# A gated delta rule loop: a second buffer for a unit's score blocks, longer delays in the rule that orders TensorE's work, keys queued ahead of values

## The chip, the cores and the metric

The kernel runs on one core of a Trainium2 chip. The metric is the device time of one execution in microseconds. The time before is the median of three runs.

## What is computed

A trunk of two layers over 1024 tokens of width 1024. Layer 0 mixes tokens with gated linear attention, layer 1 with a gated delta rule, and a dense SwiGLU network follows each. The change touches the mixer of layer 1 alone. Per chunk and head it computes this (cut from the reference):

```python
kb = kc * bc[..., None]
A = jnp.where(strict, jnp.einsum('bhid,bhjd->bhij', kb, kc) * decay, 0.0)
T = lax.linalg.triangular_solve(eye + A, eye, left_side=True, lower=True)
v_new = T @ (vc * bc[..., None]) - T @ (kb * jnp.exp(G)[..., None]) @ S
o = (qc * jnp.exp(G)[..., None]) @ S + (where(causal, qc @ kc.T * decay, 0)) @ v_new
S = jnp.exp(G_last) * S + k_dec.T @ v_new
```

There are 8 key heads, and two value heads for each. The inputs of the chunks come from projections with a short causal convolution, and the gated output goes through an output projection that is added to the residual.

## The kernel before

The mixer works in 16 **units**: a unit is one key head (its two value heads with it) over one half of the tokens, 512 of them in four chunks of 128. Units 0 to 7 are the first half, 8 to 15 the second. One unit goes through these steps, each a small generator in the code:

- `keys` and `values` project and convolve q, k and two blocks of v; `late` projects the gate z. A projection is 24 matmuls of 512 columns with split weights (`whi`, `wlo`; GpSimd makes `wlo` in L169).
- `prep` makes the decays and the score blocks `nt` (L834 to L843: four matmuls of k with itself, `pp<-k`, then eight VectorE operations), and the blocks `at` for the output.
- `solve` inverts the diagonal 32 by 32 blocks of `nt`. It sends them through DRAM (`d1`, L866) into the tile `nbx` (L868), lets VectorE do 31 steps of two operations (L883, L885), and sends the result through DRAM (`d2`, L893) into `xt` (L896). There is one `nbx` and one `xt`.
- `join` builds the whole inverse `tt` from the blocks: a transposition on VectorE (`xd`, L906), four groups of matmuls (`pq<-xd,nt` first, `pq<-ya,rr` last) with copies or additions between them, the last in L934. It reads `nt`, which until then cannot be overwritten.
- `seq` runs the four chunks in order through the state; `post` normalizes the output (L1035), transposes it (`pq<-cst,o`) and gates it; `out` projects it.

`prep` asks for the event `joined[n - 1]` before it makes `nt`, of which there is one buffer. So the score blocks of a unit are begun after the unit ahead has been joined.

What sets the order: TensorE's instructions stand in the order in which the class `Order` records them. It keeps a clock that each recorded matmul moves forward by a set amount. The strands `seq`, `post`, `join`, `prep`, `inputs` and `solve` are asked first, in this order; a strand that has yielded a number of microseconds or an event is skipped until the clock is there. When none can go on, the strand `dense` (the projections) gives one piece of three matmuls. So each `yield 1.5` says how long the rule supposes that the other engines take. The other engines and the DMA queue get their order from the framework's scheduler, which follows on from TensorE's. Every engine works through its own list in order.

Of the kernel before, what the change touches and what calls it, by code (L numbers as in the profile page):

```python
# [14 lines left out]
F32 = mybir.dt.float32  # L15
# [7 lines left out]
P = 128  # L23
# [72 lines left out]
class Trunk:  # L96
# [482 lines left out]
    def gdn(self):  # L579
# [5 lines left out]
        with ExitStack() as es:  # L585
# [75 lines left out]
            O = self.order  # L661
# [84 lines left out]
            def dense():  # L746
                yield from keys(0)
                yield from values(0)
                yield from late(0)
                yield from keys(1)  # L750
                yield from late(1)
                yield from keys(2)
                yield from values(1)
                for m in range(1, UN):
                    yield from values(m + 1)
                    if m + 2 in (NQ, UN):
                        yield from late(m + 1)
                        O.set(free[1 if m + 2 == NQ else 2])
                        yield from out(m - 1)
                        if m + 2 == NQ:  # L760
                            yield ready[1]
                            yield from keys(NQ)
                    else:
                        yield from keys(m + 2)
                        yield from out(m - 1)
                        yield from late(m + 1)
                yield ready[2]
                yield from self.headparts(1, mx, ("v", "v", "raw"))
                yield from out(UN - 1)
# [34 lines left out]
            def prep(n):  # L804
                half, hq = divmod(n, NQ)
                u = U[n]
                yield gated[half]
                gt = gts[half]
                yield keyed[n]
                yield from norms(n)  # L810
                yield 4.0
                q, k = u["q"], u["k"]

                dec = mx.tile([P, 2, C, P], F32, name="dec", tag="t1")
                up = self.upper.unsqueeze(1).to_broadcast([P, C, P])
                for h2 in range(2):
                    rhs = []
                    for nm in ("ghi", "glo"):
                        gs = gt[nm].bitcast(F32)[:, :, 2 * hq + h2:2 * hq + h2 + 1].to_broadcast([P, C, P])
                        rh = mx.tile([P, C, P], F32R, name="rh", tag="t2", bufs=2)  # L820
                        G.tensor_tensor(out=rh, in0=up, in1=gs, op=ALU.mult)
                        rhs.append(rh)
                    yield 3.0
                    ps = self.prepps()
                    psv = cview(ps)
                    self.mm(psv, self.cut, self.gt.unsqueeze(1).to_broadcast([P, C, P]), True, False)
                    self.mm(psv, self.gt, rhs[0], False, False)
                    self.mm(psv, self.gt, rhs[1], False, True)
                    S.activation(dec[:, h2].rearrange("p c i -> p (c i)"), ps, AF.Exp)
                yield 1.5  # L830
                if n:
                    yield joined[n - 1]

                nt = mx.tile([P, 8, P], F32, name="nt", tag="nt")  # L834
                pk = self.prepps()
                for c in range(C):
                    sl = slice(c * P, (c + 1) * P)
                    self.mm(pk[:, sl], k[:, sl], k[:, sl])
                for h2 in range(2):
                    for c in range(C):  # L840
                        V.scalar_tensor_tensor(out=nt[:, h2 * C + c, :], in0=pk[:, c * P:(c + 1) * P],
                                               scalar=u["nb2"][:, h2, c:c + 1], in1=dec[:, h2, c, :],
                                               op0=ALU.mult, op1=ALU.mult)  # L843
                O.set(scored[n], 4.0)
                u["nt"] = nt
                yield 2.0
                if n >= 2:
                    yield passed[n - 2]
                u["at"] = at = mx.tile([P, 8, P], F32, name="at", tag="at", bufs=2)
                ps = self.prepps()  # L850
                for c in range(C):
                    sl = slice(c * P, (c + 1) * P)
                    self.mm(ps[:, sl], k[:, sl], q[:, sl])
                for h2 in range(2):
                    V.tensor_tensor(out=at[:, h2 * C:(h2 + 1) * C, :], in0=cview(ps), in1=dec[:, h2], op=ALU.mult)

            def solve(n):
# [16 lines left out]
                G.memset(xi, 0.0)  # L874
                for b in range(4):
                    G.memset(xi[b * B:(b + 1) * B, b::B + 4], 1.0)
                yield 6.0
                start = O.clock + 0.75
                xv = xix[:, half].rearrange("p m i -> p i m")
                for s in range(B - 1):  # L880
                    m, w = B - 1 - s, s // 4 + 1
                    tv = tmpx[:, 0:m * w].rearrange("p (i m) -> p i m", m=w)
                    V.tensor_tensor(out=tv, in0=nbx[:, s, s + 1:].unsqueeze(2).to_broadcast([P, m, w]),  # L883
                                    in1=xv[:, s:s + 1, 0:w].to_broadcast([P, m, w]), op=ALU.mult)
                    V.tensor_tensor(out=xv[:, s + 1:, 0:w], in0=xv[:, s + 1:, 0:w], in1=tv, op=ALU.add)  # L885
                    yield O.until(start + 0.75 * s)

                if n:
                    yield joined[n - 1]
# [9 lines left out]
            def join(n):  # L899
# [5 lines left out]
                xd = mx.tile([P, 8, P], F32, name="xd", tag="t3")  # L905
                V.transpose(xd.rearrange("p a b -> p (a b)"), xt.rearrange("p a b -> p (a b)"))  # L906
                S.copy(tt, xt)
                yield 2.5

                rr = mx.tile([P, 8, P], F32, name="rr", tag="t4")  # L910

# [8 lines left out]
                for h2 in range(2):  # L920
                    S.copy(rr[:, hs[h2], :], quad(nt, xd, h2))
                    yield 0.5
                yield 1.5
                for h2 in range(2):
                    V.tensor_tensor(out=up(tt, h2, 96), in0=up(tt, h2, 96), in1=quad(rr, xt, h2, n=96), op=ALU.add)
                    yield 0.5
                yield 1.5
                ya = mx.tile([96, 8, P], F32, name="ya", tag="t3")
                for h2 in range(2):
                    S.copy(up(ya, h2, 96), quad(rr, tt, h2, n=96))  # L930
                    yield 0.5
                yield 1.2
                for h2 in range(2):
                    V.tensor_tensor(out=up(tt, h2, 64), in0=up(tt, h2, 64), in1=quad(rr, ya, h2, kn=96, n=64), op=ALU.add)  # L934
                U[n]["tt"] = tt
                O.set(joined[n], 1.5)

            def seq(n):
                half, hq = divmod(n, NQ)
# [89 lines left out]
            def post(n):  # L1029
                u = U[n]  # L1030
                yield passed[n]
                o, ss = u["o"]
                rs = self.rstd(ss.rearrange("p c h -> p (c h)"), 2 * C, P)
                for h2 in range(2):
                    V.tensor_tensor(out=o[:, :, h2, :], in0=o[:, :, h2, :], op=ALU.mult,  # L1035
                                    in1=rs[:, h2:2 * C:2].unsqueeze(2).to_broadcast([P, C, P]))
                yield 5.0
                yield gating[n]
                u["oT"] = []
                for h2 in range(2):  # L1040
                    ps = self.seqps()
                    self.turn(ps, lambda c: o[:, c, h2, :])
                    u["oT"].append(self.gateout(mx, h2, ps, self.gdnw, u["z"][:, h2, :]))
                O.set(posted[n], 4.0)
# [347 lines left out]
```

## Time and profile before

| | us |
|---|---|
| time, median of 3 runs (3480.7 to 3481.96) | 3481.23 |
| the profiled execution | 3478.09 |
| its span, first to last instruction | 3476.3 |
| the delta rule mixer, from the first score blocks to the last transposed output | 1347.6 to 2767.7 |
| one unit, from one join to the next, in the steady part | 85.2 to 89.2 |

The profiled execution is 1.8 us longer than its span and 3.1 us under the median. Times in the rows count from the start of the span. TensorE appears as PE (matmuls) and PEld (weight loads), VectorE as DVE, ScalarE as ACT, GpSimd as POOL, the DMA queue of SyncE as SP or SPq.

### The profile page before, as it was taken

Reading aid. Unit: us, or ns where it says so; the run is one execution under the profiler, and the core shown is the slowest. Engines: PE = TensorE matmul, PEld = TensorE weight load, DVE = VectorE, ACT = ScalarE, POOL = GpSimd, SP = SyncE. Lnnn points to the kernel's source line nnn. Section 1 sums busy time; section 2 is a strip of 40 time slices with the busy share of each in tenths; the row PEclk is TensorE's granted clock in tenths of the full one; section 3 lists DMA queues with packets and bytes.
Section 4 is the critical chain, followed back from the end, with each engine's and each line's share of the span. In section 5 each row is a group of like instructions: output and inputs, shape, how many; then the busy total and the mean of one; then the engine's idle time right before and its main releaser. Section 6 shows DMA issues by size and latency. Waiting matters only on the chain.

```text
span 3476.3 us, 40951 instructions
## 1 busy us (share of the span) xinstructions
PE 3016.6 (87%) x14547; PEld 2482.9 (71%) x14547; DVE 2065.9 (59%) x4212; ACT 1390.3 (40%) x2513; POOL 1522.6 (44%) x1037
## 2 busy tenths in 40 slices
PE   7988999799998988688888885888888879999898
PEld 5877877588876776566666674666667758888676
DVE  6465565623229866666666677666666463232888
ACT  4354444433433335343333453444443433433333
POOL 4344444455548744133223232333333345555875
PEclk9999999899999999799999998999999989999899
DMA  3221222322224202122222121222222232221431
GB/s 123 73 62 49 73 61 85 104 85 79 85 70 158 88 21 80 32 56 57 60 60 59 49 69 43 59 61 64 58 61 60 82 89 86 85 81 55 147 126 55
DMA packets 364923, 256.39 MB, mean 74 GB/s; under 512 B 67848, under 2 KB 309967, under 8 KB 364719
## 3 DMA queue, kind: packets, MB, share of 16 engines
q1 hardware_dynamic: 364654, 253.77, 24.4%
q8 instruction: 114, 1.87, 0.2%
q14 instruction: 91, 0.74, 0.1%
q0 software_dynamic: 64, 0.02, 0.0%
HBM read 219.12 MB, written 34.60 MB: 73 GB/s over the span
## 4 chain that ended last, share of the span: by engine, by line
PE 63%; DVE 26%; issue 4%; DMA 3%; ACT 2%; POOL 1%; SPq 1%; DVEq 0%; POOLq 0%; ACTq 0%
PE pd L201 36%; PE pq L201 14%; PE pp L201 8%; DVE tmpx L883 4%; DVE xix L885 3%; DVE alo L1274 2%; DVE h L1284 1%; DVE s L1268 1%; PE pp L207 1%; DVE v L692 1%; PE pp L484 1%; PE pq L207 1%; DVE k L692 1%; DMA ra<-act 1%; DVE q L692 1%
## 5 line engine op out<-in xcount | busy, mean ns | idle before, releaser
L169 POOL TENSOR_TENSOR wlo<-raw,whi 128x1024 fp32r<-128x1024 f32 x204 | 489.8, 2403 | 855.1 <-ACT whi L168 837.4
L201 PE MATMUL pd<-xhi,whi 128*128 128x512 f32 x1072 | 458.6, 428 | 1.2 <-ACT part L1082 0.9
L201 PE MATMUL pd<-xhi,wlo 128*128 128x512 f32 x1072 | 431.1, 402 | 1.9 <-POOL wlo L169 1.9
L201 PE MATMUL pd<-xlo,whi 128*128 128x512 f32 x1072 | 428.2, 399 | 0.0
L168 ACT CAST whi<-raw 128x1024 fp32r<-128x1024 f32 x204 | 213.1, 1045 | 229.7 <-PE pd L201 117.5
L1118 POOL TENSOR_TENSOR olo<-s,ohi 128x512 fp32r<-128x512 f32 x152 | 196.0, 1291 | 206.3 <-ACT ohi L1117 206.3
L1118 POOL TENSOR_TENSOR olo<-raw,ohi 128x512 fp32r<-128x512 f32 x138 | 190.7, 1384 | 201.4 <-ACT ohi L1117 177.3
L201 PEld LDWEIGHTS pd<-xhi,wlo 128*128 128x128 f32 x1072 | 206.8, 193 | 50.0 <-POOL wlo L169 2.8
L201 PEld LDWEIGHTS pd<-xhi,whi 128*128 128x128 f32 x1072 | 207.5, 194 | 36.9 <-ACT part L1082 2.0
L201 PEld LDWEIGHTS pd<-xlo,whi 128*128 128x128 f32 x1072 | 207.9, 194 | 35.6
L201 PE MATMUL pd<-whi,ohi 128*128 128x512 f32 x384 | 171.0, 446 | 43.5 <-DVE h L316 23.1
L1117 ACT CAST ohi<-s 128x512 fp32r<-128x512 f32 x152 | 94.3, 622 | 231.3 <-PE pd L201 174.7
L883 DVE TENSOR_TENSOR tmpx<-nbx,xix 128x60 f32<-128x60 f32 (+24 forms) x496 | 177.7, 358 | 8.5
L316 DVE TENSOR_TENSOR h<-h,pd 128x512 f32<-128x512 f32 x192 | 130.8, 683 | 62.9 <-PE pd L201 62.8
L1117 ACT CAST ohi<-raw 128x512 fp32r<-128x512 f32 x138 | 85.1, 621 | 197.6 <-POOL olo L1118 176.6
L201 PE MATMUL pd<-wlo,ohi 128*128 128x512 f32 x384 | 163.7, 426 | 0.0
L201 PE MATMUL pd<-whi,olo 128*128 128x512 f32 x384 | 161.8, 421 | 0.9 <-DVE olo L346 0.9
L885 DVE TENSOR_TENSOR xix<-xix,tmpx 128x60 f32<-128x60 f32 (+24 forms) x496 | 153.2, 309 | 8.7
L201 PE MATMUL pq<-xd,nt 128*128 128x128 f32 x256 | 57.3, 400 | 114.0 <-DVE xd L906 114.0
L1274 POOL TENSOR_TENSOR blo<-t,bhi 128x1536 fp32r<-128x1536 f32 (+1 forms) x32 | 124.7, 3896 | 57.4 <-ACT bhi L1273 53.0
L1226 DVE TENSOR_TENSOR p<-p,pp 128x512 f32<-128x512 f32 x38 | 26.1, 688 | 195.9 <-DMA raw<-in_ffn_w_gate_up_dram 148.3
L201 PE MATMUL pd<-bhi,ahi 128*128 128x512 f32 x264 | 108.3, 410 | 39.2 <-DVE h L1284 24.5
(393 smaller groups left out, 8261.2 us busy)
## 6 DMA issues: line engine op xcount, KB each, us to landing
raw<-in_gdn_w_in_dram SPq DMA_DIRECT2D x96, 512.0 KB, 4.0
raw<-in_ffn_w_gate_up_dram SPq DMA_DIRECT2D x176, 256.0 KB, 3.3
raw<-in_gla_w_in_dram SPq DMA_DIRECT2D x48, 512.0 KB, 3.8
ra<-act SPq DMA_DIRECT2D x88, 256.0 KB, 4.9
rb<-in_ffn_w_down_dram SPq DMA_DIRECT2D x24, 768.0 KB, 6.2
raw<-in_gdn_w_out_dram SPq DMA_DIRECT2D x32, 512.0 KB, 3.8
act<-p SPq DMA_DIRECT2D x44, 256.0 KB, 2.0
act<-u SPq DMA_DIRECT2D x38, 256.0 KB, 2.0
```

Source lines behind the costliest of these rows:

```text
L168: nc.scalar.copy(hi, raw)
L169: nc.gpsimd.tensor_tensor(out=lo, in0=raw, in1=hi.bitcast(F32), op=ALU.subtract)
L201: self.nc.tensor.matmul(out, lhsT, rhs, start=start, stop=stop, **kw)
L207: self.nc.tensor.transpose(ps[:, c * P:(c + 1) * P], src(c), self.ident)
L316: self.nc.vector.tensor_tensor(out=o, in0=o, in1=ps, op=ALU.add)
L484: TE.matmul(ps[:, sl], d[:, sl], d[:, sl], start=True, stop=True)
L692: V.scalar_tensor_tensor(out=out, in0=raw[:, s:s + HT], scalar=tap(s), in1=out, op0=ALU.mult, op1=ALU.add)
L883: V.tensor_tensor(out=tv, in0=nbx[:, s, s + 1:].unsqueeze(2).to_broadcast([P, m, w]), in1=xv[:, s:s + 1, 0:w].to_broadcast([P, m, w]), op= ...
L885: V.tensor_tensor(out=xv[:, s + 1:, 0:w], in0=xv[:, s + 1:, 0:w], in1=tv, op=ALU.add)
L1117: self.nc.scalar.copy(hi, src)
L1118: eng.tensor_tensor(out=lo, in0=src, in1=hi.bitcast(F32), op=ALU.subtract)
L1274: eng.tensor_tensor(out=lo, in0=src, in1=hi.bitcast(F32), op=ALU.subtract)
```

## The change

It does four things, all in the function of the delta rule mixer.

1. `nt` gets two buffers, and `prep` of unit n asks for `joined[n - 2]` where it asked for `joined[n - 1]`.
2. The numbers in `solve`, `join` and `post` grow: 6.0 to 9.0 before the steps, 0.75 to 1.1 for a step, 2.5 to 4.0 behind the transposition, 1.5 to 2.5 twice and 1.2 to 2.5 inside the join, 1.5 to 2.5 behind it, 5.0 to 8.0 ahead of the output's transpositions. This alters no instruction, only where TensorE's stand.
3. In the strand `dense`, `values(m + 1)` moves from the first to the third place of a round, behind the keys of unit m + 2 and the output projection of unit m - 1 (not in the last round of a half).
4. Nothing is added or removed: every engine does the same operations.

```diff
                 for m in range(1, UN):
-                    yield from values(m + 1)
                     if m + 2 in (NQ, UN):
+                        yield from values(m + 1)
                         yield from late(m + 1)
...
                         yield from keys(m + 2)
                         yield from out(m - 1)
+                        yield from values(m + 1)
                         yield from late(m + 1)
...
-                if n:
-                    yield joined[n - 1]
+                if n >= 2:
+                    yield joined[n - 2]
-                nt = mx.tile([P, 8, P], F32, name="nt", tag="nt")
+                nt = mx.tile([P, 8, P], F32, name="nt", tag="nt", bufs=2)
...
-                yield 6.0
-                start = O.clock + 0.75
+                yield 9.0
+                start = O.clock + 1.1
...
-                    yield O.until(start + 0.75 * s)
+                    yield O.until(start + 1.1 * s)
...
-                O.set(joined[n], 1.5)
+                O.set(joined[n], 2.5)
...
-                yield 5.0
+                yield 8.0
                 yield gating[n]
```

From line 763 on, the changed file's line numbers are higher by one.

TensorE's list before, at the end of the join of unit 4: the last group of the join, the transposed values and keys of that unit, and behind them the score matmuls `pp<-k` of unit 5.

```order
L201 MATMUL pq<-ya,rr 64x64 x8
L207 MATMUL pp<-cst,v_13533 128x128 x4
L207 MATMUL pp<-cst,v_13622 128x128 x4
L207 MATMUL pq<-cst,k 128x128 x4
L201 MATMUL pp<-k 128x128 x4
```

TensorE's list after: the score matmuls of unit 6 stand inside the first group of the join of unit 5, a whole join earlier, and the transposed outputs (`pq<-cst,o`) of unit 4 directly behind.

```order
L201 MATMUL pq<-xd,nt 128x128 x4
L201 MATMUL pp<-k 128x128 x4
L201 MATMUL pq<-xd,nt 128x128 x4
L207 MATMUL pq<-cst,o 128x128 x8
L201 MATMUL pd<-xhi,whi 128x512
```

The score matmuls have moved by one join; in the second half of the tokens they stand directly ahead of that first group in some units.

VectorE's list before, from the transposition of the solved blocks to the first step of the next solve:

```order
L906 STREAM_TRANSPOSE xd<-xt 128x1024
L925 TENSOR_TENSOR tt<-tt,pq 96x4x96 x2
L934 TENSOR_TENSOR tt<-tt,pq 64x4x64 x2
L961 TENSOR_TENSOR vt<-pp,sk 128x512 x2
L841 SCALAR_TENSOR_TENSOR nt<-pp,nb_13984,dec 128x128 x8
L855 TENSOR_TENSOR at<-pp,dec 128x512 x2
L999 COPY gstate_9876<-pq 128x256
...
L883 TENSOR_TENSOR tmpx<-nbx,xix 128x31
```

VectorE's list after, over the same stretch:

```order
L907 STREAM_TRANSPOSE xd<-xt 128x1024
...
L1036 TENSOR_TENSOR o<-o,rs_y 128x4x128 x2
L692 SCALAR_TENSOR_TENSOR v_14014<-raw,col_conv,v_14014 128x512
L842 SCALAR_TENSOR_TENSOR nt<-pp,nb_13797,dec 128x128 x8
L344 SCALAR_TENSOR_TENSOR sz<-pq,col_rest,sz 128x512 x2
...
L856 TENSOR_TENSOR at<-pp,dec 128x512 x2
L926 TENSOR_TENSOR tt<-tt,pq 96x4x96 x2
L935 TENSOR_TENSOR tt<-tt,pq 64x4x64
L884 TENSOR_TENSOR tmpx<-nbx,xix 128x31
```

The score blocks of the next unit now stand ahead of the join's additions, and the next solve's first step stands between the last two of them. Between the transposition and the join's first addition there were no VectorE operations before; now the rest of the output's work, the values' convolutions and both score tiles are there.

## Rows read from the trace of the kernel before

**Rows 1.** The page: busy time of TensorE, share of the span, instructions; and the chain that ended last, by engine.

```profile
PE 3016.6 (87%) x14547; PEld 2482.9 (71%) x14547; DVE 2065.9 (59%) x4212; ACT 1390.3 (40%) x2513; POOL 1522.6 (44%) x1037
...
PE 63%; DVE 26%; issue 4%; DMA 3%; ACT 2%; POOL 1%; SPq 1%; DVEq 0%; POOLq 0%; ACTq 0%
```

**Rows 2.** Busy time by stretch, each from the end of one join to the next: two steady units of the first half, the passage from the first half to the second, a steady unit of the second half. Columns: stretch, its length, busy us of PE, PEld, DVE, ACT and POOL with counts, granted TensorE clock as a share of the full one, DMA share, GB/s.

```profile
1648.70:1737.40 88.70, 73.08 (x369) 60.25 (x368) 57.89 (x154) 34.59 (x75) 26.41 (x30) 0.90 0.21 58
1737.40:1826.10 88.70, 73.09 (x369) 60.22 (x367) 57.93 (x153) 34.53 (x75) 26.38 (x30) 0.90 0.22 58
...
2000.00:2119.80 119.80, 86.48 (x430) 72.05 (x429) 77.46 (x204) 50.64 (x96) 35.57 (x32) 0.84 0.21 56
...
2378.90:2466.60 87.70, 74.07 (x369) 61.42 (x369) 57.45 (x155) 35.10 (x77) 26.41 (x26) 0.88 0.22 59
```

**Rows 3.** The last operation of a join (L934, two for each of 16 units): the line's own view (duration minimum, median, maximum in ns, first and last start), and from the timeline the second operation of units 1, 7 and 8 (start, us).

```profile
L934 DVE TENSOR_TENSOR tt<-tt,pq x32: 351/412/414, 1408.5 to 2727.0; 64x256 f32<-64x256 f32 x32
...
1472.00 0.41 DVE L934 TENSOR_TENSOR tt<-tt,pq 64x256 f32<-64x256 f32 x1 [0.22 <-PE pq L201]
...
1999.65 0.35 DVE L934 TENSOR_TENSOR tt<-tt,pq 64x256 f32<-64x256 f32 x1
...
2119.43 0.41 DVE L934 TENSOR_TENSOR tt<-tt,pq 64x256 f32<-64x256 f32 x1 [0.22 <-PE pq L201]
```

**Rows 4.** One round on VectorE, from the join of unit 4 to that of unit 5 (timeline: start, us, with the idle time before it in brackets).

```profile
1736.49 0.88 DVE L934 TENSOR_TENSOR tt<-tt,pq 64x256 f32<-64x256 f32 x2 [6.99 <-PE pq L201]
...
1739.57 2.16 DVE L841 SCALAR_TENSOR_TENSOR nt<-pp,nb,dec 128x128 f32<-128x128 f32 x8 [0.73 <-PE pp L201]
...
1755.68 0.18 DVE L883 TENSOR_TENSOR tmpx<-nbx,xix 128x31 f32<-128x31 f32 x1
...
1794.44 0.17 DVE L885 TENSOR_TENSOR xix<-xix,tmpx 128x8 f32<-128x8 f32 x1
...
1806.84 1.25 DVE L906 STREAM_TRANSPOSE xd<-xt 128x1024 f32<-128x1024 f32 x1
1816.34 0.55 DVE L925 TENSOR_TENSOR tt<-tt,pq 96x384 f32<-96x384 f32 x1 [8.26 <-ACT sz L720]
...
1825.21 0.88 DVE L934 TENSOR_TENSOR tt<-tt,pq 64x256 f32<-64x256 f32 x2 [6.99 <-PE pq L201]
```

**Rows 5.** The DMA queue in the same round (timeline: start, us of issue), and the median us from issue to landing of two of its transfers over the stage.

```profile
1741.76 1.81 SPq L866 DMA_DIRECT2D d<-nt  x4
1744.88 1.71 SPq L868 DMA_DIRECT2D nbx<-d  x4
...
1794.64 2.52 SPq L893 DMA_DIRECT2D d<-xix  x4
1798.59 1.83 SPq L896 DMA_DIRECT2D xt<-d  x4
...
nbx<-d SPq DMA_DIRECT2D x64, 128.0 KB, 2.7
...
xt<-d SPq DMA_DIRECT2D x64, 32.0 KB, 1.9
```

**Rows 6.** TensorE's waits in the stage: who it waited for, us in total, times, the longest.

```profile
PE pq L201 <- DVE xd L906: 114.0, 16, 24.6
PE pq L207 <- DVE o L1035: 56.1, 14, 4.3
PE pd L201 <- DVE h L316: 23.1, 9, 3.7
PE pq L201 <- DVE rt L976: 22.7, 16, 1.8
...
PE pq L201 <- DVE gstate L1003: 9.0, 7, 1.3
```

**Rows 7.** VectorE's costliest groups in the stage (count, busy us, mean ns of one, idle before them), and its waits for `rt` and the values' convolution.

```profile
L883 DVE TENSOR_TENSOR tmpx<-nbx,xix 128x60 f32<-128x60 f32 (+24 forms) x496 | 177.7, 358 | 8.5
L885 DVE TENSOR_TENSOR xix<-xix,tmpx 128x60 f32<-128x60 f32 (+24 forms) x496 | 153.2, 309 | 8.7
L692 DVE SCALAR_TENSOR_TENSOR v<-raw,col_conv,v 128x512 f32<-128x512 f32 x96 | 85.3, 888 | 40.1 <-ACT v L690 39.0
L316 DVE TENSOR_TENSOR h<-h,pd 128x512 f32<-128x512 f32 x120 | 81.7, 683 | 39.6 <-PE pd L201 39.4
...
DVE rt L976 <- PE pq L201: 45.3, 30, 4.8
...
DVE v L692 <- ACT v L690: 39.0, 14, 3.4
```

**Rows 8.** VectorE beside GpSimd at two places of that round (timeline): a step of the solve and one of GpSimd's weight operations, then one of the small root operations (L251), the output's normalization (two operations) and another weight operation.

```profile
1756.93 0.19 DVE L885 TENSOR_TENSOR xix<-xix,tmpx 128x29 f32<-128x29 f32 x1
1757.15 2.35 DVE L883 TENSOR_TENSOR tmpx<-nbx,xix 128x28 f32<-128x28 f32 x1
...
1757.06 2.40 POOL L169 TENSOR_TENSOR wlo<-raw,whi 128x1024 fp32r<-128x1024 f32 x1 [4.97 <-ACT whi L168]
...
1786.09 0.16 DVE L251 SCALAR_TENSOR_TENSOR rs_y<-rs_t,rs_y 128x8 f32<-128x8 f32 x1
...
1786.32 3.44 DVE L1035 TENSOR_TENSOR o<-o,rs_y 128x512 f32<-128x512 f32 x2
...
1786.27 2.34 POOL L169 TENSOR_TENSOR wlo<-raw,whi 128x1024 fp32r<-128x1024 f32 x1 [7.00 <-ACT whi L168]
```

More of the change, by code (lines that the diff above doesn't have):

```diff
@@ L907, in join @@
                 S.copy(tt, xt)
-                yield 2.5
+                yield 4.0
                 rr = mx.tile([P, 8, P], F32, name="rr", tag="t4")
@@ L922, in join @@
                     yield 0.5
-                yield 1.5
+                yield 2.5
                 for h2 in range(2):
@@ L926, in join @@
                     yield 0.5
-                yield 1.5
+                yield 2.5
                 ya = mx.tile([96, 8, P], F32, name="ya", tag="t3")
@@ L931, in join @@
                     yield 0.5
-                yield 1.2
+                yield 2.5
                 for h2 in range(2):
```

## The prediction

> **What bounds the kernel now.** The page comes first [rows 1]. TensorE is busy for 87% of the span, and the chain that ended last is TensorE's for 63% and VectorE's for 26%. That is a mean over stages, so the stage that the change touches is read by itself. Cut from join to join, it shows the same picture again and again [rows 2]: 88.7 us for a unit of the first half, 87.7 for one of the second, of which TensorE is busy 73.1 at a granted clock of 0.90, VectorE 57.9, ScalarE 34.5, GpSimd 26.4. No engine is full. TensorE's 73.1 us at 0.90 would be 65.8 at the full clock. So something goes round in 88.7 us that is no engine's work.
>
> The timeline of one round shows what it is [rows 4, 5]. The join of unit 4 ends at 1737.4. Then come the next score blocks (1739.6 to 1741.7), their way through DRAM (issues at 1741.8 and 1744.9, the last landing 2.7 us behind its issue), the solve's steps from 1755.7 to 1794.6, the way back (1794.6 and 1798.6), the transposition at 1806.8 to 1808.1, and the join's matmuls and additions until 1826.1. The next score blocks wait for this, because they overwrite the one buffer that the join reads. It is one ring: 2.2 to the blocks, 2.2 for them, 13.9 until the first step, 38.9 of steps, 12.3 until the transposition, 1.2, and 18.0 for the join; the sum is 88.7. TensorE's waits agree: the longest is for the transposed blocks, 114.0 us in 16 times [rows 6]. It is less than the whole slack because TensorE runs slowly while there is slack.
>
> **The change part by part.**
>
> The second buffer takes the score blocks out of the ring. They and their transfers can run while the unit ahead is being joined. That would remove 2.2 + 2.2 + 13.9 = 18.3 us from each round, if they are ready in time. In VectorE's new list they stand behind the transposition and the output's normalization: some 9 us of VectorE work ahead of them (the last state step, a dozen small root operations at 0.16, 3.4 us of normalization [rows 8], four or five convolutions at 0.9 [rows 7] in part), then 2.2 us, then 7.3 us until the last piece has landed (1741.7 to about 1749 [rows 4, 5]). This is 18.5 us beside a join of 18.0, so they are just in time, and the next solve, which stands right at the join's end in the list, can begin there.
>
> What is late next: the solve itself and the join, still in a ring, since there is one `nbx` and one `xt`. I add the new round from VectorE's list. (a) From the join's end to the solve's last step stand the 62 steps, (177.7 + 153.2)/16 = 20.7 us [rows 7], and some 12 us of other work: six convolutions of keys at 0.8 to 0.9, four residual additions at 0.68 [rows 7], and a dozen operations of `seq` at about 0.35. Together 32.7, against 38.9 before. (b) Then about 10 us of VectorE work to the transposition; the transfers need from 1794.6 to about 1802, 7.4 us [rows 5], and lie beside it. (c) The transposition, 1.25. (d) TensorE's list has the output's transpositions of the unit ahead in front of the first group of the join in most units, and these wait for the normalization that follows the transposition on VectorE: 2 + 3.4 = 5.4 us. (e) The join: its matmuls have 42 to 60 large matmuls and both score groups among them in the new list, where 39 to 42 stood, so I take 20 instead of 18. The sum is 69.4. (f) Between VectorE and TensorE remain the handshakes of `seq`, which now meet longer blocks of steps. VectorE waits for `rt` 45.3/16 = 2.8 us a unit now [rows 7]; I take 3.5. That makes **73 us a round**.
>
> Its bounds. Below: TensorE's work at the full clock, 65.8 us, if every handshake is hidden. Above: 80 us, which is the second rival. I take 73 as it is the sum of durations seen in the trace and lies between the floors of both engines and the present round.
>
> The longer delays cost no instruction. The output's transpositions wait 56.1 us in 14 times now [rows 6], but this wait ends ahead of the wait for the transposed blocks and is hidden under it: worth nothing by itself before, and in the new round it is term (d). In the join they give VectorE and ScalarE room and are term (e).
>
> Keys ahead of values: the values' two projections move behind the keys' two and the output projection, each with 24 matmuls, its weight load, two splitting operations, three convolution operations of VectorE and three of ScalarE. The values' convolutions now fall into the join, where VectorE idles 8.3 + 7.0 of 18 us [rows 4]. I cost them at nothing. If that cover is gone, the transposition of v waits as the convolution does now, 39.0/14 = 2.8 us [rows 7], up to 3 in a unit. The weights of these projections are queued on the same DMA queue as `d1`, `nbx`, `d2` and `xt`. What stands behind `d2` there is first used by TensorE around the join's first group, so a queue that waits for the solve holds up nothing that is needed earlier; a late load would cost 4 us and its two splitting operations. GpSimd clears blocks of `nt` when `d1` has landed and is idle for 62 of 88.7 us; its weight operations behind that have room.
>
> Where it counts: joins 1 to 7 take 1472.4 to 2000.0, joins 8 to 15 2119.8 to 2727.4 [rows 3], that is 527.6 + 607.6 = 1135.2 us for 13 rounds, 87.3 each. At 73 they take 949: **186 us less**. The passage between the halves (119.8 us [rows 2]) waits for the second half's inputs, which the change doesn't touch, and stays; so do the first rounds (63 us from join 0 to join 1) and the tail. Since the first rounds of the second half have their score blocks early, they may gain some 15 us more, and a longer tail may take as much; I leave both out. From the profiled execution, 3478.1 - 186 = 3292; the median stands 3.1 higher, **3295 us**.
>
> **A rule against this.** First the rows: a step of the solve that takes 0.19 us takes 2.35 when it begins 0.1 us behind a GpSimd weight operation, and ends with it; the same happens to the normalization [rows 8]. So part of VectorE's 57.9 us is standing still, and steps put closer together meet more of GpSimd's 26.4 us. The Trainium skill ("SBUF — State Buffer", section "SBUF: two separate sides") states it as an exclusive lock: a VectorE operation with two SBUF inputs and a GpSimd operation that reads SBUF block each other for the whole instruction. The trace agrees at these places (2.35 beside 2.40). Its consequence is the second rival.
>
> **The rivals.**
>
> 1. *TensorE becomes the bound.* All of VectorE's handshakes are hidden and the clock stays up: 66 us a round, 13 x 21.3 = 277 less, 3204. For it: the slow clock of 0.90 comes with the waits. Against: VectorE's list leaves little slack, 57.9 and more of 66.
>
> 2. *VectorE and GpSimd exclude each other.* The steps take 20.7 us a unit by their mean, where 62 at about 0.22 would take 13.6 (the undisturbed ones have 0.17 to 0.19 [rows 4, 8], wider ones more); with the normalization and the convolutions I put the standing still at 11 us. So VectorE alone needs about 47; if all of GpSimd's 26.4 falls beside it, the two need 73, and the waits of VectorE that cannot be filled (some 7 us of `rt` and convolutions) come on top: 80 a round, 13 x 7.3 = 95 less, 3386. It decides once nearly every weight operation meets VectorE. Against: many VectorE operations read PSUM, and 30.8 us of idle time are there to be used.
>
> 3. *The buffer is not what is waited for.* The blocks are made earlier but the solve starts as late, since the list puts other work ahead, or `nbx` lands late. Then a round keeps 85 to 87.3 us: 3451 to 3481.
>
> 4. *Slower.* In VectorE's new list the steps stand in blocks of up to 20, 20 x 0.334 = 6.7 us, ahead of `rt` and the state's update, and TensorE, bound to its own list, has only nine projection matmuls, about 2.1 us, between two links of `seq`. If all six links of a unit met such a block, TensorE would stand 6 x 4.6 = 27.6 us on top of 65.8: 93.4 a round, 13 x 6.1 = 79 more, 3560. It decides when TensorE's waits for `rt` and the state pass 21.5 us a unit; now they are (22.7 + 9.0)/16 = 2.0 [rows 6]. For it: the blocks are there in the list. Against: I count two or three such meetings in a unit, not six.
>
> **How the numbers follow.** The forecast has 0.63, rival 1 0.08, rival 2 0.17, rival 3 0.05, rival 4 0.07. The forecast's own range is 69 to 77 us a round, 3243 to 3347. The range takes in rival 1's time and rival 2's: 3200 to 3400. Changes under 0.2% (7 us) cannot be told from none. Faster: the forecast, rivals 1 and 2 and a little of rival 3, 0.89. Same: the rest of rival 3 and mixtures that cancel, 0.04. Slower: rival 4, 0.07.
>
> **What would show it.** Right: joins 73 us apart; score blocks of unit n + 1 written before the join of unit n ends; the first step of a solve within 2 us of a join's end; TensorE's wait for the transposed blocks well under 114 us and its clock above 0.90 in the steady rounds. Rival 1: VectorE full and TensorE without waits. Rival 2: solve steps of over 2 us eight times a unit, and VectorE's busy time up from 57.9. Rival 3: a gap of 10 us and more between join and first step. Rival 4: waits for `rt` and the state over 20 us a unit. The prediction is wrong if the round is outside 69 to 77 us, or if the passage between the halves or the tail moves by more than 20.

## The result, and the profile after

The changed kernel takes 3306.8 us (median; 3303.61 to 3309.54), the kernel before 3481.6 us in the same runs. The ratio is 0.9497, with a 95% interval of 0.9481 to 0.9514: faster by 5.0%. The prediction had 3295.

The page of the kernel after: busy time of the engines, and the chain that ended last.

```profile
PE 2980.4 (90%) x14547; PEld 2452.3 (74%) x14547; DVE 2105.8 (64%) x4212; ACT 1401.0 (42%) x2525; POOL 1527.4 (46%) x1037
...
PE 22%; DVE 11%; issue 2%; DMA 1%; ACT 1%; POOL 0%; SPq 0%; DVEq 0%; POOLq 0%; ACTq 0%
```

Against [rows 1] TensorE's busy time has moved little (36 us less), but its share is 90% where it was 87%: the span is 3305.3 us, 171.0 less. The shares of the chain sum to far less than 100% here, so it isn't used. The stage is read from join to join again.

Busy time by stretch of the kernel after, columns as in [rows 2]: the rounds of units 5, 6 and 7, the passage to the second half (unit 8), the round behind it, and one of the steady rounds of the second half (unit 13).

```profile
1691.30:1762.50 71.20, 64.85 (x355) 54.24 (x354) 53.27 (x137) 35.42 (x74) 24.52 (x27) 0.98 0.28 73
1762.50:1840.00 77.50, 70.71 (x373) 58.35 (x373) 64.27 (x155) 38.15 (x78) 27.30 (x30) 0.96 0.26 67
...
1840.00:1916.50 76.50, 67.19 (x355) 54.56 (x353) 61.30 (x153) 33.63 (x81) 23.65 (x22) 0.96 0.21 54
...
1916.50:2056.00 139.50, 114.30 (x557) 94.18 (x556) 110.35 (x277) 63.17 (x114) 51.15 (x46) 0.90 0.24 65
2056.00:2112.10 56.10, 48.29 (x273) 40.00 (x273) 48.76 (x151) 24.18 (x62) 11.96 (x16) 0.94 0.21 55
...
2332.20:2411.20 79.00, 71.21 (x373) 58.46 (x372) 58.95 (x155) 37.20 (x78) 27.70 (x26) 0.96 0.31 77
```

A steady round is 70 to 79 us, where it was 85 to 89. TensorE fills 88 to 91% of it in these rows, at a granted clock of 0.96 to 0.98 (before 0.88 to 0.90). Joins 1 and 7 end at 1481.0 and 1916.5, joins 8 and 15 at 2056.0 and 2553.5, so 13 rounds take 435.5 + 497.5 = 933.0 us, 71.8 each (before 87.3). The passage is 139.5 us, where it was 119.8, and the round behind it only 56.1.

One round on VectorE in the kernel after, unit 6 (timeline): the score blocks of unit 6, the last operations of the join of unit 5 with the first steps of the solve, a step beside GpSimd, the last step, the transposition, and the end of the join of unit 6.

```profile
1746.50 2.15 DVE L842 SCALAR_TENSOR_TENSOR nt<-pp,nb,dec 128x128 f32<-128x128 f32 x8
...
1761.63 0.41 DVE L935 TENSOR_TENSOR tt<-tt,pq 64x256 f32<-64x256 f32 x1 [7.01 <-PE pq L201]
1761.97 0.18 DVE L884 TENSOR_TENSOR tmpx<-nbx,xix 128x31 f32<-128x31 f32 x1
1762.10 0.41 DVE L935 TENSOR_TENSOR tt<-tt,pq 64x256 f32<-64x256 f32 x1
...
1763.99 2.38 DVE L884 TENSOR_TENSOR tmpx<-nbx,xix 128x54 f32<-128x54 f32 x1
...
1798.58 0.17 DVE L886 TENSOR_TENSOR xix<-xix,tmpx 128x8 f32<-128x8 f32 x1
...
1810.49 1.23 DVE L907 STREAM_TRANSPOSE xd<-xt 128x1024 f32<-128x1024 f32 x1
...
1839.10 0.41 DVE L935 TENSOR_TENSOR tt<-tt,pq 64x256 f32<-64x256 f32 x1 [6.02 <-PE pq L201]
1839.57 0.41 DVE L935 TENSOR_TENSOR tt<-tt,pq 64x256 f32<-64x256 f32 x1
```

GpSimd beside that long step (timeline):

```profile
1763.92 2.37 POOL L169 TENSOR_TENSOR wlo<-raw,whi 128x1024 fp32r<-128x1024 f32 x1 [5.74 <-ACT whi L168]
```

The score blocks are done 13.9 us ahead of the join, and the solve starts between the join's two last operations, where it began 18.3 us behind them [rows 4]. The same round on TensorE, small matmuls alone (timeline):

```profile
1818.79 1.03 PE L207 MATMUL pq<-cst,o 128*128 128x128 f32 x8
1819.66 1.06 PE L201 MATMUL pq<-xd,nt 128*128 128x128 f32 x8
1820.55 1.06 PE L201 MATMUL pp<-k 128*128 128x128 f32 x8
```

The transposed blocks were ready at 1811.7, and TensorE came to them at 1819.66, with no idle time directly in front: it was still busy with projections. Not every round is like this one: over the eight steady rounds TensorE comes to the blocks 5.0 us after they are ready in the mean, and in units 12 to 14 it is there at once (0.1 us). TensorE's waits in the stage (1260 to 2600 us), columns as in [rows 6]:

```profile
PE pq L201 <- DVE rt L977: 24.7, 20, 3.0
PE pq L201 <- DVE gstate L1004: 21.6, 13, 4.0
...
PE pq L201 <- DVE gstate L1000: 7.5, 5, 2.8
...
PE pq L207 <- DVE o L1036: 6.4, 4, 2.9
...
PE pq L201 <- DVE xd L907: 4.1, 4, 2.4
```

The wait for the transposed blocks was 114.0 us [rows 6] and is 4.1; that for the output's normalization was 56.1 and is 6.4. The largest that are left are the handshakes of `seq` (`rt` and the state `gstate`), 53.8 us of the 154 that TensorE is idle from 1260 to 2600 us.

### The profile page after: what moved, and what is told of

The parts are those of the page before. It is cut to its first block, busy times and chain, and to the rows that moved or that the text cites. A ratio compares the mean times of both kernels' runs of the same rounds, so it can differ in the third digit from the quotient of the medians.

```text
span 3305.3 us, 40855 instructions
## 1 busy us (share of the span) xinstructions
PE 2980.4 (90%) x14547; PEld 2452.3 (74%) x14547; DVE 2105.8 (64%) x4212; ACT 1401.0 (42%) x2525; POOL 1527.4 (46%) x1037
## 5 line engine op out<-in xcount | busy, mean ns | idle before, releaser
L201 PE MATMUL pd<-xhi,whi 128*128 128x512 f32 x1072 | 450.6, 421 | 1.0 <-ACT part L1083 0.7
L1119 POOL TENSOR_TENSOR olo<-raw,ohi 128x512 fp32r<-128x512 f32 x138 | 190.6, 1383 | 202.2 <-ACT ohi L1118 177.9
L886 DVE TENSOR_TENSOR xix<-xix,tmpx 128x60 f32<-128x60 f32 (+24 forms) x496 | 168.5, 340 | 13.1
L884 DVE TENSOR_TENSOR tmpx<-nbx,xix 128x60 f32<-128x60 f32 (+24 forms) x496 | 159.5, 322 | 26.3 <-DMA nbx<-d 13.5
L201 PE MATMUL pd<-bhi,ahi 128*128 128x512 f32 x264 | 108.7, 412 | 36.4 <-DVE h L1285 20.1
L1275 POOL TENSOR_TENSOR blo<-rb,bhi 128x1536 fp32r<-128x1536 f32 (+1 forms) x24 | 97.8, 4074 | 42.6 <-ACT bhi L1274 42.6
```

The costliest lines, as they stand in the source:

```text
L201: self.nc.tensor.matmul(out, lhsT, rhs, start=start, stop=stop, **kw)
L1119: eng.tensor_tensor(out=lo, in0=src, in1=hi.bitcast(F32), op=ALU.subtract)
L1275: eng.tensor_tensor(out=lo, in0=src, in1=hi.bitcast(F32), op=ALU.subtract)
```

## The experiments

Ratios are against the kernel before, run beside each. Differences between two experiments are of medians taken at different times, between which the kernel before itself moved from 3476.4 to 3481.6, so 5 us of such a difference say nothing. "Start" is the solve's first step, counted from the end of the join ahead. Means of the eight steady rounds (units 4 to 7 and 12 to 15) from the timelines, us:

| | blocks written, from join ahead | start | steps | to `xd` | `xd` to join end | round | mean of 13 rounds |
|---|---|---|---|---|---|---|---|
| before | +4.8 | 18.2 | 38.7 | 11.3 | 18.0 | 87.5 | 87.3 |
| buffer alone | +4.5 | 20.1 | 32.5 | 11.1 | 18.3 | 83.4 | 82.6 |
| buffer, keys | +3.8 | 14.6 | 36.9 | 10.9 | 19.8 | 83.4 | 76.6 |
| and solve's delays | -9.5 | 4.6 | 30.5 | 12.8 | 28.7 | 77.8 | 72.9 |
| and join's delays instead | -0.5 | 13.1 | 30.1 | 11.4 | 21.7 | 77.6 | 72.1 |
| after | -12.8 | -0.6 | 36.3 | 12.6 | 25.5 | 75.0 | 71.8 |
| longer delays | -17.1 | -6.2 | 35.1 | 11.6 | 33.0 | 74.8 | 71.6 |

The transposition itself (1.2 us) is the part of a round that the columns leave out.

**Which part of the change.** Theory A: the buffer only permits an early start, and the solve's longer delays, which set the order, make it. Theory B: the buffer alone is enough. Four kernels build the change up.

Buffer alone (edits of before):

```diff
-                if n:
-                    yield joined[n - 1]
+                if n >= 2:
+                    yield joined[n - 2]
-                nt = mx.tile([P, 8, P], F32, name="nt", tag="nt")
+                nt = mx.tile([P, 8, P], F32, name="nt", tag="nt", bufs=2)
```

> The kernel before with the second buffer and the event of two units back alone; old delays, old place of the values. Theory A (the buffer permits, the solve's delays do it: in TensorE's list of this kernel the next score matmuls still stand behind the join in the steady units, 16 to 21 us of TensorE work behind the join's first group): steady rounds stay at 83 to 88 us, only the first units of each half gain; 3420 to 3470. Rival B (the buffer is the whole gain): rounds of 72 us, 3300 to 3330.

Measured: 3426.7 us, 0.9856 (0.9839 to 0.9872), 50 us of the 175 and inside theory A's range. In the steady rounds the score blocks still come 4.5 us behind the join, though nothing holds them there any more. TensorE's small matmuls at the end of a join show why (timeline of this kernel, lines of 1706 to 1712 us):

```profile
1706.12 1.15 PE L201 MATMUL pq<-ya,rr 96*64 96x64 f32 x16
...
1709.39 0.60 PE L207 MATMUL pp<-cst,v 128*128 128x128 f32 x4
...
1711.70 0.50 PE L201 MATMUL pp<-k 128*128 128x128 f32 x3
```

The score matmuls are still listed behind the join's last group. What the buffer gives comes from a shorter run of steps (32.5 for 38.7, other work having moved out of it) and from early rounds, and long rounds of 125.8 and 120.4 us (units 3 and 10) take part of it back.

Keys ahead of values as well:

```diff
                 for m in range(1, UN):
-                    yield from values(m + 1)
                     if m + 2 in (NQ, UN):
+                        yield from values(m + 1)
...
                         yield from out(m - 1)
+                        yield from values(m + 1)
```

> Buffer and keys ahead of values, old delays. Theory A: the score matmuls stand 15 us of TensorE work behind the join's first group, so the old ring is still there through TensorE's list; rounds 83 to 88 us, 3410 to 3470. Rival B: 3300 to 3330. Rival C (keys ahead of values carry half of the gain): about 3390.

Measured: 3380.4 us, 0.9719 (0.9704 to 0.9733), 46 us less. The steady round is the same 83.4, as theory A expected, but the time is 30 us under that theory's range and nearest to rival C's. The gain is in the long rounds: unit 3's falls from 125.8 to 89.0, and unit 10's from 120.4 to 42.0 (unit 11's rises from 72.1 to 110.9). With the buffer alone the blocks of unit 3 come 48.9 us behind the join ahead, here 17.5. The passage grows from 128.1 to 147.1 us. In a steady round the blocks still follow the join (VectorE, timeline):

```profile
1681.04 0.40 DVE L935 TENSOR_TENSOR tt<-tt,pq 64x256 f32<-64x256 f32 x1
1682.03 0.40 DVE L935 TENSOR_TENSOR tt<-tt,pq 64x256 f32<-64x256 f32 x1
...
1684.32 2.16 DVE L842 SCALAR_TENSOR_TENSOR nt<-pp,nb,dec 128x128 f32<-128x128 f32 x8 [1.23 <-PE pp L201]
...
1696.41 0.18 DVE L884 TENSOR_TENSOR tmpx<-nbx,xix 128x31 f32<-128x31 f32 x1
```

Buffer and keys, with the delays of `solve` alone:

```diff
-                yield 6.0
-                start = O.clock + 0.75
+                yield 9.0
+                start = O.clock + 1.1
...
-                    yield O.until(start + 0.75 * s)
+                    yield O.until(start + 1.1 * s)
```

> Buffer, keys ahead, and of the longer delays those of the solve alone (9.0 and 1.1); join and post keep the old ones. Theory A: the score matmuls stand beside the join's first group as in the changed kernel, so nearly all of the gain is there, 3300 to 3330. Rival D (the join's longer delays matter as much, since TensorE else waits inside the join): 3350 to 3400.

Measured: 3324.8 us, 0.956 (0.9545 to 0.9574), inside theory A's range. Buffer and keys, with the delays of `join` and `post` alone:

```diff
-                yield 2.5
+                yield 4.0
...
-                yield 1.5
+                yield 2.5
...
-                yield 1.5
+                yield 2.5
...
-                yield 1.2
+                yield 2.5
...
-                O.set(joined[n], 1.5)
+                O.set(joined[n], 2.5)
...
-                yield 5.0
+                yield 8.0
```

> Buffer, keys ahead, and of the longer delays those of the join and post alone; the solve keeps 6.0 and 0.75. Theory A: like buffer and keys alone within 20 us, 3410 to 3470, as the score matmuls again stand 14 to 18 us behind the join's first group. Rival D: 3350 to 3400.

Measured: 3317.6 us, 0.9538 (0.9524 to 0.9552). Of the 74 us between the second kernel and the kernel after, the solve's delays alone give 56 and those of join and post alone 63. Theory A expected 3410 to 3470 us of the second half, and rival D's range of 3350 to 3400 is missed by both halves, so both theories fall. VectorE's timeline of this kernel, the same join as above:

```profile
1678.78 2.14 DVE L842 SCALAR_TENSOR_TENSOR nt<-pp,nb,dec 128x128 f32<-128x128 f32 x8
1680.85 0.73 DVE L935 TENSOR_TENSOR tt<-tt,pq 64x256 f32<-64x256 f32 x2
...
1694.08 0.18 DVE L884 TENSOR_TENSOR tmpx<-nbx,xix 128x31 f32<-128x31 f32 x1
```

The blocks are now just ahead of the join's end, and the steps take 30.1 us instead of 36.9. The solve's delays reach the same round in another way: a start 10 us earlier, and a later join. In the last four rows of the table the start moves over 19 us, and the round stays at 75 to 78; what the start gains stands again in the steps and between `xd` and the join's end. This says that something else than the ring bounds these rounds; the next experiments test it.

**Is the solve's ring the bound?** Every second step of the solve is left out, in the kernel before and in the kernel after.

```diff
+                    if s % 2 == 0:
-                    V.tensor_tensor(out=tv, in0=nbx[:, s, s + 1:].unsqueeze(2).to_broadcast([P, m, w]),
+                        V.tensor_tensor(out=tv, in0=nbx[:, s, s + 1:].unsqueeze(2).to_broadcast([P, m, w]),
...
-                    V.tensor_tensor(out=xv[:, s + 1:, 0:w], in0=xv[:, s + 1:, 0:w], in1=tv, op=ALU.add)
+                        V.tensor_tensor(out=xv[:, s + 1:, 0:w], in0=xv[:, s + 1:, 0:w], in1=tv, op=ALU.add)
```

> The kernel before, with every second of the solve's 31 steps left out (16 stay, so the inverse is not the whole one); TensorE's list and all delays as before. Ring theory (a round of the kernel before is a latency that runs through the solve): some 10 us go from each of 16 rounds, 140 to 180 us less, about 3320. Rival (TensorE's work sets the round before): under 40 us less, above 3440.

Measured: 3302.3 us, 0.9493 (0.9478 to 0.9508), 176 us less. The steps' stretch falls from 38.7 to about 18, the round from 87.3 to 76.1, and TensorE's wait for the transposed blocks from 114.0 us in 16 times to 18.8 in 2 (TensorE's waits of this kernel, columns as in [rows 6]):

```profile
PE pq L201 <- DVE xd L907: 18.8, 2, 17.2
```

The ring does bound the kernel before, and below 76 something else does.

> The changed kernel with the same steps left out, TensorE's list and delays as in the changed kernel. If TensorE's list with its handshakes sets the new round (in the trace of after its wait for the transposed blocks is gone, and some 7 us a unit of waits for rt and the state are left): 30 to 80 us less than the changed kernel, 3225 to 3275. Rival (the solve is still in the ring, only shorter): 130 to 160 us less, about 3160.

Measured: 3226.3 us, 0.927 (0.9249 to 0.929), 80 us less than after. The stretch of steps falls to 13 to 18 us in the steady rounds, from 36 in the mean, the round only to 67.5 from 71.8. The transposed blocks are then ready 21 to 29 us before TensorE's list comes to them in the steady rounds, as in unit 6 (timelines of VectorE and TensorE):

```profile
1759.50 1.24 DVE L908 STREAM_TRANSPOSE xd<-xt 128x1024 f32<-128x1024 f32 x1
...
1783.89 1.06 PE L201 MATMUL pq<-xd,nt 128*128 128x128 f32 x8
```

Of the 20 us taken out, 4 reach the round.

Longer delays in the kernel after (9.0 to 10.0, 1.1 to 1.2):

```diff
-                yield 9.0
-                start = O.clock + 1.1
+                yield 10.0
+                start = O.clock + 1.2
...
-                    yield O.until(start + 1.1 * s)
+                    yield O.until(start + 1.2 * s)
```

> The changed kernel with the solve's delays longer still, 10.0 and 1.2 for 9.0 and 1.1: in TensorE's list the next score matmuls stand 5 to 7 us ahead of the join's first group in most steady units, where they stand within 4 us of it now. If TensorE's list sets the round: within 10 us of the changed kernel, 3297 to 3317. If the solve's ring sets it: 20 to 50 us less.

Measured: 3304.9 us, 0.95 (0.9484 to 0.9517), the same as after. The solve starts 5.6 us earlier and the join ends as late.

**VectorE beside GpSimd.** In the kernel after, GpSimd makes the low part of half a weight tile only, in this mixer; the products of the other half use the first half's low parts.

```diff
         nc.scalar.copy(hi, raw)
+        if getattr(self, "short", False):
+            n = shape[1] // 2
+            lo = lo[:, 0:n]
+            nc.gpsimd.tensor_tensor(out=lo, in0=raw[:, 0:n], in1=hi[:, 0:n].bitcast(F32), op=ALU.subtract)
+            return hi, lo
...
```

> The changed kernel, in which GpSimd makes the low part of a weight tile for half of it alone in this mixer (1.2 instead of 2.4 us each; the second half of the products uses the first half's low parts, so the projections are not exact). If VectorE's standing still beside GpSimd is on the path that sets the round: 5 us a round, 70 to 80 less, about 3230. If TensorE's list sets it and VectorE only matters at the handshakes: 10 to 40 us less, 3265 to 3295. If neither: 3300 to 3310.

Measured: 3217.9 us, 0.9242 (0.922 to 0.9264), 89 us less than after and a little more than the first of the three expectations; the round is 66.7. Busy time of 200 us of this kernel, then of the kernel after:

```profile
1650.00:1850.00 200.00, 188.82 (x1026) 156.94 (x1025) 155.49 (x446) 100.08 (x222) 48.59 (x75) 0.99 0.28 74
```

```profile
1650.00:1850.00 200.00, 183.21 (x991) 151.88 (x991) 158.13 (x417) 96.34 (x199) 70.69 (x79) 0.97 0.27 70
```

VectorE runs 446 operations where it ran 417, in less time. TensorE gets through 35 more matmuls and its clock is 0.99. Of its waits, `rt` goes from 24.7 to 12.0 us and the state from 29.1 to 15.1. Solve steps of over 1 us take 47.6 us where they took 95.9. That GpSimd delivers the low parts sooner explains little: TensorE waited 4.7 us in all for them in the kernel after, and waits 0.4 here. The whole stage, from 1260 us to the last transposed output, in this kernel and then in the kernel after:

```profile
1260.00:2508.00 1248.00, 1152.26 (x6178) 958.37 (x6177) 916.25 (x2613) 623.95 (x1304) 311.04 (x454) 0.96 0.27 70
```

```profile
1260.00:2596.00 1336.00, 1182.79 (x6183) 974.16 (x6182) 1018.31 (x2613) 623.11 (x1304) 454.20 (x454) 0.94 0.25 66
```

Of the 88 us between them, TensorE is busy 30.5 less and idle 57.5 less.

The same cause with nothing left out: VectorE makes every second low part of this mixer, GpSimd the others.

```diff
-        nc.gpsimd.tensor_tensor(out=lo, in0=raw, in1=hi.bitcast(F32), op=ALU.subtract)
+        self.turns = getattr(self, "turns", 0) + 1
+        eng = nc.vector if getattr(self, "short", False) and self.turns % 2 else nc.gpsimd
+        eng.tensor_tensor(out=lo, in0=raw, in1=hi.bitcast(F32), op=ALU.subtract)
...
```

> The changed kernel with every second low part of a weight tile in this mixer made by VectorE (about 1.4 us each, from two operations of 512 at 0.69) instead of GpSimd (2.4 us). If VectorE's standing still costs as much as its own work: 9.6 us less of GpSimd gains 5.6 a unit and 5.5 more of VectorE loses most of it, 3290 to 3315. Rival: VectorE's longer list holds up the handshakes of seq, over 3330.

Measured: 3239.8 us, 0.9318 (0.9305 to 0.9331), 67 us less than after and faster than both kernels; my expectation was too cautious. The groups of the low parts in this kernel (columns as in [rows 7]):

```profile
L171 DVE TENSOR_TENSOR wlo<-raw,whi 128x1024 fp32r<-128x1024 f32 x67 | 85.9, 1282 | 13.2 <-ACT whi L168 12.1 <-PE pp L209 0.7 <-ACT raw L686 0.2
```

```profile
L171 POOL TENSOR_TENSOR wlo<-raw,whi 128x1024 fp32r<-128x1024 f32 x67 | 163.9, 2447 | 334.8 <-ACT whi L168 322.1 <-issue 6.4 <-DMA nbx<-d 3.3
```

One such operation costs VectorE 1.28 us of its own time. On GpSimd it takes 2.45 us, and VectorE stood beside it for up to as long: solve steps of over 1 us are 44 in the kernel after (95.9 us) and 24 here (48.7 us). From 1260 us to the last transposed output VectorE's operations without these subtractions take 921.7 us, 96.6 less than in the kernel after. The mean round is 68.3.

**The output's delay alone**, in the kernel before (5.0 to 8.0 in `post`):

```diff
-                yield 5.0
+                yield 8.0
                 yield gating[n]
```

> The kernel before with one number changed, 8.0 for 5.0 ahead of the output's transpositions, so that TensorE reaches them later and need not wait (56.1 us in 14 times before). If that wait was hidden under the ring, as the prediction says: within 7 us of the kernel before, 3470 to 3485, and the 56 us turn up as a longer wait for the transposed blocks. If it was on the path: 30 to 56 us less.

Measured: 3468.5 us, 0.9968 (0.9955 to 0.998), 9 us less. TensorE's waits in the stage:

```profile
PE pq L201 <- DVE xd L906: 150.4, 16, 23.0
...
PE pq L207 <- DVE o L1035: 17.9, 12, 4.1
```

The wait for the normalization falls from 56.1 to 17.9 us, and the wait for the transposed blocks grows from 114.0 to 150.4: 36 of the 38 us turn up there, and some 9 us reach the end.

**The passage as before**, in the kernel after: the second unit of the second half asks for the join of the first again.

```diff
-                if n >= 2:
+                if n == NQ + 1:
+                    yield joined[n - 1]
+                elif n >= 2:
                     yield joined[n - 2]
```

> The changed kernel, where unit 9 alone asks for the join of unit 8 as in the kernel before, so that its scores stand behind unit 8's join in TensorE's list. If the longer passage between the halves in the changed kernel (139.5 us from join 7 to join 8, 119.8 before) is work of unit 9 done early: the passage falls to 118 to 128, the next round grows from 56 to 65 to 75, and the time stays within 10 us, 3297 to 3317. If the passage is a loss: 15 to 20 us less.

Measured: 3307.6 us, 0.9507 (0.9494 to 0.952), no difference from after. Its passage and the round behind it (windows):

```profile
1916.40:2039.90 123.50, 105.87 (x519) 86.87 (x518) 93.61 (x218) 60.68 (x111) 46.16 (x38) 0.93 0.25 67
2039.90:2129.60 89.70, 76.77 (x407) 63.73 (x407) 78.25 (x215) 40.07 (x81) 31.52 (x33) 0.94 0.25 66
```

16 us come off the passage and 33.6 go onto the next round, more than expected (it was to grow to 65 to 75), and the rounds behind make up the difference: unit 11's falls from 90.2 to 52.1, unit 12's grows from 76.8 to 91.9. The longer passage of the kernel after is work of unit 9 done early.

**GpSimd's small operations.** The tiles `rh` of `prep` are made by 16 ScalarE operations, in the kernel after.

```diff
-                        G.tensor_tensor(out=rh, in0=up, in1=gs, op=ALU.mult)
+                        for c in range(C):
+                            S.activation(rh[:, c, :], self.upper, AF.Copy,
+                                         scale=gt[nm].bitcast(F32)[:, c, 2 * hq + h2:2 * hq + h2 + 1])
```

> The changed kernel with the four masked gate tiles of a unit (rh, 4.3 us of GpSimd a unit) made by ScalarE in 16 operations of about 0.3 us. By the run with half the weight operations (9.6 us less of GpSimd a unit gave 5.6 us a unit), 4.3 should give 2.5, 40 us in all: 3260 to 3280. Rival: ScalarE's 5 us more a unit lengthen the handshakes of seq by as much, 3300 to 3330.

Measured: 3311.4 us, 0.9518 (0.9503 to 0.9533), no gain. TensorE now waits for `rh`: 32.8 us in 27 times, where it waited 3.5 in 8 for GpSimd's. That wait is near the gain that was expected; that it is what took the gain was not tried.

## Why the prediction was right, and where not

The sum was made for the profiled execution: 3478.1 - 186 = 3292. That execution took 3307.1. The difference of 15 us comes from these terms:

| term | predicted, us | measured, us |
|---|---|---|
| 13 rounds | -186 | 933.0 - 1135.2 = -202.2 |
| passage between the halves | 0 | 139.5 - 119.8 = +19.7 |
| first two joins | 0 | +5.2 and +3.4 |
| tail of the mixer, from the last join to the last output's normalization | 0 | 37.1 - 40.3 = -3.2 |
| behind that normalization | 0 | +6.1 |
| sum | -186 | -171.0 |

The mark 2767.7 of the time before is the end of that normalization. Taken to the last transposed output (2768.4 before, 2596.0 after), the tail gains nothing (+1.5) and what is behind it loses 1.4.

- **What bounds the kernel before: right.** Halving the steps took 176 us, and the round fell by 11.2 us for 20 us of steps taken out: the ring was the bound down to a floor near 76.
- **The new round: right in size.** 73 predicted, 75.0 in the steady rounds, 71.8 over all 13. By terms: (a) and (f) together 36.2 predicted, 35.7 measured from the join's end to the last step; (b) 10 against 12.6; (c) 1.25 against 1.2; (d) and (e) together 25.4 against 25.5. The mean is lower than the steady rounds through the early ones (49.8, 56.1, 53.0 us for units 2, 9 and 10), which the prediction had put at some 15 us, left out. The nearness of the mean is in part luck: the eight steady rounds give 100 us where 73 a round would give 116, and the other five (units 2, 3, 9, 10 and 11) give 102 where it would give 70.
- **"The second buffer takes the score blocks out of the ring": half wrong.** With the buffer alone the blocks stay where they were (+4.5 us), and so does the solve's start. That is the mechanism of rival 3 in the steady rounds, though not its price: its rounds of 85 to 87.3 us and 3451 to 3481 are not reached, with 83.4 and 3426.7. The buffer permits, TensorE's list decides. My forecast was read from the new list, so the number came out; the 18.3 us were credited to the wrong part.
- **"Keys ahead of values: at nothing": wrong.** With the buffer it is worth 46 us, all in the irregular rounds. What it is worth without the buffer was not tried.
- **"The longer delays cost no instruction" and are terms (d) and (e): too small.** On top of buffer and keys they are worth some 74 us, 8 x 8.4 = 67 of it in the steady rounds, and either half of them brings most of that. Why the join's delays shorten the run of steps by 7 us is read from the order of VectorE's work, not isolated.
- **The output's wait "worth nothing by itself": nearly.** 9 us of 38.
- **The new bound: not seen.** The prediction kept a ring through VectorE. The halved steps and the longer delays show that the ring has slack now; in the round shown TensorE reaches the join's first group 8 us late. The term for the join had the right length for another reason, since it holds TensorE's lateness and not the longer list inside the join alone. What is left of a steady round is TensorE's own work, 68.1 of the 75.0 us at a granted clock of 0.97, and 6.9 us of idle time, in which the handshakes of `seq` are the largest part. This is the neighbourhood of rival 1; 66 us a round would need all handshakes hidden.
- **Rival 2: its mechanism is there, its size not.** The kernel after has the same standing still as before (44 steps of over 1 us, 49 before), and the round didn't go to 80. But it is on the path: with GpSimd's low parts halved 89 us go, with half of them on VectorE 67. The step of 2.38 us in the round shown began 0.07 us behind a GpSimd weight operation of 2.37 us and ended 0.08 us behind it. It is no single case: of the 39 solve operations of the kernel after that begin well inside such an operation (0.05 us or more behind its start, 0.3 or more ahead of its end), 38 end 0.03 to 0.15 us behind its end. The exclusive lock that the prediction takes from the Trainium skill ("SBUF — State Buffer", section "SBUF: two separate sides") agrees with these rows. The prediction's 20.7 - 13.6 = 7.1 us a unit of standing still in the steps is somewhat large: with a median operation of 0.24 us, the 49 long ones (104.9 us) make some 5.8 a unit before, and 5.3 after, by my estimate.
- **Rival 4: small.** The waits for `rt` and the state are (24.7 + 21.6 + 7.5)/16 = 3.4 us a unit, against 2.0 before and 21.5 where it would have decided.
- **The passage: wrong.** It was to stay, and moved by 19.7 us, almost the bound of 20 that was set. The run with the old order there shows that this is moved work and worth nothing in the sum.

Open: how the 89 us of the halved low parts divide. TensorE's idle time accounts for some 57, of which 27 are waits for `rt` and the state, and its shorter busy time for some 30; what VectorE has to do with the rest was not separated. Why either half of the delays alone brings most of their gain is open too. What a mixer without any low part on GpSimd would take was not tried.

## What to carry to other kernels

A second buffer removes a dependency, not a place in a list: where one engine's order is fixed, look where the freed instructions stand in it before crediting the buffer. When a ring is shortened, take the next bound from an experiment that makes the ring much shorter still; here half the steps gave 176 us before the change and 80 after it. An engine far from full can still be on the path through another: a gain left here was to give a busy VectorE more work, since the same work on GpSimd held it up longer.

## What the hardware showed that I had not expected

In the run that shares the low parts a subtraction of 128 x 1024 elements takes 1.28 us on VectorE and 2.45 us on GpSimd, and moving 67 of them to VectorE (86 us of its time) made the kernel 67 us faster. VectorE's busy time over the whole kernel fell a little, from 2105.8 to 2097.3 us, though it ran 67 operations more.
